# A two-layer decoder trunk on one core: second products of exact pairs contracted over all 128 rows instead of 64

## The chip, the core and the metric

The kernel runs on one core of a Trainium2 chip. The metric is the device time of one execution in microseconds (us); lower is better. TensorE does the matrix products, VectorE (DVE) and ScalarE (ACT) work on elements, GpSimd (POOL) does the rest of the element work, and SyncE (SP) issues most of the transfers.

## The reference, cut to what matters

A trunk of two layers on 1024 tokens of 1024 channels. The even layer projects the normed input and runs an RWKV-7 time mix, an S5 state space and an attention over 256 memory tokens; the odd layer runs a Mamba-2 branch, a latent attention (MLA) of 8 heads and the memory attention again. The three places that the change touches:

```python
# RWKV: decay and in-context rate from two latents of 64 channels each
log_w = -jax.nn.softplus(-(w0 + jnp.tanh(w_lat) @ w2)) - 0.5
iclr = jax.nn.sigmoid(a0 + a_lat @ a2)
...
# latent attention: scores of a block of 128 queries, 128 plain and 64 rotary channels a head
sc = (jnp.einsum('bqhd,bkhd->bhqk', q_nope[:, start:end], k_nope[:, :end])
      + jnp.einsum('bqhr,bkr->bhqk', q_pe[:, start:end], k_pe[:, :end]))
...
# memory attention: 4 heads of 64 channels, 256 keys
sc = jnp.einsum('bqhd,bmhd->bhqm', q, k).astype(jnp.float32) * HEAD_DIM ** -0.5
```

## The kernel before

**Exact pairs.** Float32 data are split into two parts, `hi + lo`, each short enough for TensorE's one-pass format (float32r). `split` (L402) does it with a copy on ACT (L404) and a subtraction on DVE (L405). A full product of 128 contracted rows is then three products: hi by hi, lo by hi, hi by lo.

Where the contraction has only 64 rows, one tile holds both parts: 64 of its 128 rows hold hi and the other 64 hold lo. Against a second tile that holds the hi part of the other factor in both halves, a single product over 128 rows gives hi by hi plus lo by hi. A second product adds hi by lo: in the kernel before it runs over the 64 rows that hold hi alone. Three places do so:

- LoRA of the RWKV branch (`rw_prep0`, L590 to L592): the latents `lt` against the weights `l2h` and then `l2l`, for two banks `pw` and `pa`. One unit is a head pair and half of the tokens; there are 16 units, so 32 second products of 64 rows and 512 columns. `lora` (L925 to L932) makes `l2h` with one copy on ACT and `l2l` with two subtractions on DVE of 64 rows by 128 (L931).
- Memory keys of the odd layer (`mem_branch` with `exact`, L1126 to L1135): queries `mqp` against `mkh` and then `mkr`. Eight rounds of (channel tile, half of the tokens, head), each with four pairs of 256 columns: 32 second products. `mkr` is made by two subtractions on DVE of 64 rows by 512 (L1097).
- Rotary part of the latent attention's scores (`mla_scores`, L2205): each bank gets `qnh` by `knh`, `qnh` by `knl`, `qnl` by `knh`, then `qp` by `kph` and, over 64 rows, `qp` by `kpl`. 64 blocks of 128 queries, the keys in one to three pieces: 104 second products of 128 to 512 columns. `kph` and `kpl` come from `split_load` and are full tiles.

**Order.** `Flow` (L159) is a planner that runs while the kernel is built. Streams of work share TensorE, each yields what its next step waits for, and the planner keeps its own clock: a product costs its columns at 2400 columns per us, whatever its rows are. The order of TensorE's instructions that comes out is fixed in the program. The dense projections (`dense`, L336) are one of the streams, and fill TensorE beside the RWKV branch, the memory branch and the latent attention. All matrix products have line L179 in the profile, the transposes L183, so the rows are told apart by tiles: out<-moving,stationary.

**Softmax of a block in the latent attention.** DVE adds the mask (L2210), reduces the maximum (L2211) and scales it (L2214), ACT takes the exponential (L2217), DVE the reciprocal (L2222), and ACT or DVE scales the probabilities (L2224, L2226). TensorE transposes them (`g<-ident,pe`), ACT and DVE split the result into `pth` and `ptl` (L2262, L2263), and TensorE multiplies by the values into `yps`.

**RWKV unit.** After LoRA come scans on DVE (L601) and exponentials, then triangular systems: `ga` goes to DRAM (`d_in`, L698), comes back as `ai`, one system per partition, and is inverted by chains of small POOL operations (L710, L712). The outputs pass `rw_out`, with a POOL operation on `ty` (L850) ahead of transposes on TensorE.

Of the kernel before, what the change touches and what calls it, by code (L numbers as in the profile page):

```python
# [10 lines left out]
F32 = mybir.dt.float32  # L11
F32R = mybir.dt.float32r
# [7 lines left out]
P = 128  # L20
# [9 lines left out]
# ---------------------------------------------------------------- host layout  # L30
# [24 lines left out]
def host_arrays(inp):  # L55
# [5 lines left out]
    # the S5 channels of a tile: by channel in the group, then by group  # L61
# [26 lines left out]
    # rows 32 r + q, column 2 c + i: channel q of group 2 r + i of tile c  # L88
# [23 lines left out]
    # by head pair, for both halves of the rows  # L112
# [46 lines left out]
class Flow:  # L159
    """The order of TensorE's work. Streams (generators) share it: the first one in rank that is  # L160
    ready goes on by a step. A stream yields what its next step waits for: a time in us from now,
    a PSUM tag and a number of its buffers, the name of an event, or a list of these."""
# [8 lines left out]
    # TensorE, in the order of the calls  # L171
# [13 lines left out]
    # PSUM buffers  # L185
# [11 lines left out]
    # events  # L197
# [27 lines left out]
    def run(self, until):  # L225
        """until the given streams have ended"""
# [19 lines left out]
class Item:  # L246
    """One product of the dense chain: out[m, tokens] = w^T x as three products of exact parts.
    x(h): (hi, lo) [128, kt, 512]; evac(h, psum) takes a half of the tokens. gen: any other work instead"""
# [8 lines left out]
class Tiles(list):  # L257
    """tiles [128, n], indexed as one [128, k, n] would be"""
# [6 lines left out]
class K:  # L265
# [4 lines left out]
    # ------------------------------------------------------------ constants  # L270
    def consts(self, es):
# [22 lines left out]
        # 1 - mu  # L294
# [10 lines left out]
    def new_banks(self, g, yps):  # L305
        """banks besides the dense chain's two"""
        if hasattr(self, "psum2"):
            self.psum2.close()
        self.psum2 = ExitStack()
        self.es.push(self.psum2)  # L310
        self.pbank = self.psum2.enter_context(self.tc.tile_pool(name="psum2", bufs=1, space=PSUM))
        self.flow.set_banks("g", g)
        self.flow.set_banks("yps", yps)
# [6 lines left out]
    # ------------------------------------------------------------ dense  # L320
    def load_w(self, parts, src, kt, m=P, pool=None):
        """generator: exact parts of a weight tile [128, kt, m], in pieces; yields the end of each"""
# [14 lines left out]
    def dense(self, items):  # L337
        """generator: the chain of dense products, the weights of the next ones loaded ahead"""
# [17 lines left out]
        def fill(n):  # L356
            """weights of the items up to the next but one, as far as there is room"""
            while at[0] < min(n, len(items) - 1) or live[0] < WB and at[0] < min(n + 2, len(items) - 1):
                at[0] = next(todo)
# [42 lines left out]
    def split(self, hi, lo, src):  # L402
        """hi + lo = src exactly, each with float32r's significand"""
        self.nc.scalar.copy(hi, src)  # L404
        self.nc.vector.tensor_tensor(lo, src, hi.bitcast(F32), A.subtract)  # L405

    def split_load(self, pool, hi, lo, src, n=HT):
        """exact parts of a DRAM tile [128, T]"""
# [5 lines left out]
    def gate2(self, g, ps):  # L414
        """g = 2 * silu(ps)"""
# [4 lines left out]
    def keep_evac(self, kind, dst):  # L420
        """evac of a projection to DRAM: 'gate', 'u' or 'copy'"""
        nc = self.nc

        def evac(h, ps):
            t = self.wp.tile([P, HT], F32, name="ev", bufs=2)
            if kind == "u":
                # tokens by place in the block, last first
# [11 lines left out]
    def put_y(self, kt, s, y):  # L439
        """y [128, n]: out-projection input kt, to DRAM"""  # L440
        self.nc.sync.dma_start(self.yd[kt, :, s], y)

    # ------------------------------------------------------------ norms
    def rstd(self, r, n, fill, scale_mat, rank_wait=0):
        """generator: r [128, n] = (mean over channels + eps)^-1/2 on every partition;
        fill(i, s): squares of one part of the channels for tokens s, or None after the last"""
# [14 lines left out]
    def norm_first(self, p, h, xhi, xlo):  # L461
        """generator: half of the input's tokens as exact parts, first without their norm (a factor per token, self.r0)
        for the products that come first, then with it"""
# [42 lines left out]
    def rw_consts(self, p):  # L506
# [16 lines left out]
        # per channel: w0 / 2, a0 / 2, 1 - k_a  # L523
# [6 lines left out]
        # identity start of the 32-row triangular inverses, in 4 interleaved column groups  # L530
        self.t0 = p.tile([P, 8, 32], F32, name="t0")
        nc.gpsimd.memset(self.t0, 0.0)
        for q in range(4):
            # t - 4 cc - q != 0 keeps 0, else 1
# [3 lines left out]
        # block diagonal holders of the inverses, zero outside what gets written  # L538
# [13 lines left out]
    def shift_evac(self, ci, dst, bd=None):  # L552
        """evac: p + (shift(p) - p) * mu, one half of the tokens each, to DRAM"""
# [15 lines left out]
    def rw_prep0(self, st, p, lat, l2, k, wk):  # L569
        """generator: channel-wise part of one head pair, one half of the tokens,  # L570
        as far as the triangular systems need it"""
# [18 lines left out]
        for i, (o, hs) in enumerate(((pw, slice(0, 64)), (pa, slice(64, 128)))):  # L590
            F.matmul(o, lhsT=l2h[:, i, :], rhs=lat[:, i], start=True, stop=False)
            F.matmul(o, lhsT=l2l[hs], rhs=lat[hs, i], start=False, stop=True)  # L592
# [23 lines left out]
        # K~, B~  # L616
        kr = wk.tile([P, 4, 2, P], F32, name="kr", bufs=3)
        nc.vector.tensor_tensor(kr[:, :, 0, :], b3(kh), e[:, :, 0:P], A.mult)
        # 1 / |k|^2, for both sides
# [5 lines left out]
        # the triangular part [s, t], transposed  # L625
# [5 lines left out]
    def pp_parts(self, x):  # L631
        """exact parts of x, where ce and cc of this unit were or will be"""
# [9 lines left out]
    def half_products(self, bm, kr, which, out):  # L642
        """out[s, b, h, t] = B~^T (K~ or R~), the latter masked to s <= t"""
# [6 lines left out]
        for h in range(2):  # L650
            if which == 0:
                # what the mask would clear is never read
# [5 lines left out]
    def rw_prep1(self, st, p, r, v, wk):  # L658
        """generator: the rest of it"""
# [6 lines left out]
        # bonus  # L666
# [3 lines left out]
        # token-major V, B~, K~'  # L670
# [18 lines left out]
    def rw_inv0(self, st, idx, wk):  # L689
        """inverses of the 32-blocks on the diagonal of I + A, one per partition,  # L690
        columns in 4 interleaved groups; transposed, into a block holder"""
# [21 lines left out]
        d_out = self.dr.tile([4, 8, 8, 4, 32], F32, name="d_out", bufs=2)  # i hb cc q t  # L713
# [5 lines left out]
    def rw_inv1(self, st, wk):  # L719
        """generator: the 32-block inverses grown to the inverse of the whole chunk"""  # L720
# [8 lines left out]
        # 32 -> 64  # L729
# [24 lines left out]
        # 64 -> 128  # L754
# [15 lines left out]
    def rw_seq(self, st, s0, i, wk):  # L770
        """generator: the chunks of one half in turn; y ends up in PSUM, token-major. i: which of the two at work"""
# [18 lines left out]
        for b in range(4):  # L790
# [33 lines left out]
            # the next chunk's start, in the scale of its middle  # L824
# [9 lines left out]
    def rw_out(self, p, hh, st, zd, wk):  # L834
        """generator: group norm (token-major), bonus, gate; result to DRAM"""
# [29 lines left out]
    def rsqrt(self, out, x, tmp, scale, eps):  # L865
        """out = (x scale + eps)^-1/2 on VectorE: a first guess from the exponent, then Newton's method"""
# [12 lines left out]
    def rw_items(self, np_, x, rd, zd, npairs=8):  # L879
        """the projections of the RWKV branch; the first two by halves of the tokens, with tiles from np_"""  # L880
# [32 lines left out]
    def rw_streams(self, cp, wk, rd, zd, npairs=8):  # L913
        """streams of the RWKV branch. The halves of two head pairs take turns, so that a half can begin
        before the one ahead of it has ended"""
# [9 lines left out]
        def lora(p):  # L925
            lr = self.pp.tile([P, 2, P], F32, name="l2", bufs=1)
            nc.sync.dma_start(lr, self.I["lora2"][p])
            l2 = (self.pp.tile([P, 2, P], F32R, name="l2h", bufs=1), self.pp.tile([P, P], F32R, name="l2l", bufs=1))
            nc.scalar.copy(l2[0], lr)
            for i, hs in enumerate((slice(0, 64), slice(64, 128))):  # L930
                nc.vector.tensor_tensor(l2[1][hs], lr[hs, i], l2[0][hs, i].bitcast(F32), A.subtract)  # L931
# [8 lines left out]
        def latents():  # L940
            """exact parts, stacked: tanh(w) hi | lo, a lo | hi; those of the first half stay"""
# [65 lines left out]
    # ------------------------------------------------------------ memory branch  # L1007
    def mem_norm(self, p, wait):
        """generator: the normed memory as exact parts, to DRAM"""
# [29 lines left out]
    def kv_items(self, layer, dst):  # L1039
        """keys (channel-major) and values of the normed memory, to dst (DRAM) [128, 4, 256]"""  # L1040
# [12 lines left out]
        # values by token: both token tiles in a bank, half of the contraction each  # L1053
# [27 lines left out]
    def mem_branch(self, layer, qd, zd, k0, p, wait, exact=False):  # L1081
        """generator: q (channel-major) and gates from DRAM -> out-projection inputs k0, k0 + 1.
        exact: products of exact parts, a head's high and low rows (or columns) side by side"""
# [5 lines left out]
        if exact:  # L1089
# [5 lines left out]
            nc.scalar.copy(kh, kl)  # L1095
            for h, hs in enumerate((slice(0, 64), slice(64, 128))):
                nc.vector.tensor_tensor(kr[hs, h], kl[hs, h], kh[hs, h].bitcast(F32), A.subtract)  # L1097
# [14 lines left out]
        def load(c, qh):  # L1112
# [3 lines left out]
            for h in range(2):  # L1116
                qs[c, qh, h] = q
                if exact:
                    # rows of the head's place high, the others low
# [4 lines left out]
        def scores(c, qh, h, q2):  # L1124
# [3 lines left out]
            for j in range(2):  # L1128
                o = slice(q2 * 256 + j * P, q2 * 256 + j * P + P)
                if exact:  # L1130
                    F.matmul(sc[:, j, :], lhsT=q[:, o], rhs=kh[:, h, c], start=True, stop=False)
                    F.matmul(sc[:, j, :], lhsT=q[hs, o], rhs=kr[hs, h, c], start=False, stop=True)
# [72 lines left out]
    def reduce_angle(self, k, out, x):  # L1205
        """out = x - 2 pi round(x / 2 pi)"""
# [7 lines left out]
    def sincos(self, s, c, r):  # L1214
        """r in [-pi, pi]; r is overwritten by its absolute value"""
# [5 lines left out]
    def s5_small(self, p):  # L1221
        """powers of the decays, e^(8 i theta)'s angle, |a|^8 and (a - 1) / lambda, to DRAM"""
# [37 lines left out]
        # f = (a - 1) / lambda  # L1260
# [25 lines left out]
    def s5_params(self, p, tp):  # L1286
# [13 lines left out]
        # b^ = f b  # L1300
        b16 = lambda ap: ap.unsqueeze(2).broadcast_to([P, 32, 16])
        # one column group more than there is: 32-wide slices of the last group stay inside
# [21 lines left out]
        # skip, as a part of the impulse response: row 32 r + q, column q  # L1324
# [9 lines left out]
    def s5_prep_x(self, q, ct, wk, st, free, wait):  # L1334
        """generator: what the state part of one 128-channel tile (8 channel groups) needs besides its input"""
# [1139 lines left out]
```

## Time and profile before

| | |
|---|---|
| median of 3 runs | 2826.01 us (2821.52 to 2829.27) |
| profiled execution, first to last instruction | 2839.6 us, 42364 instructions |
| PE busy, weight loads (PEld) busy | 2604.9 us (92%), 2058.7 us |
| DVE, ACT, POOL busy | 1787.5 us (63%), 1250.4 us (44%), 807.9 us (28%) |
| mean granted TensorE clock | 0.944 of full speed |

The page tells no more of the profiled execution than its span. The span is 13.6 us (0.5%) above the median of the runs, so stretches of it are taken as they stand and differences are carried to the median. A matmul's row shows when it starts; its end is modelled and includes the way through the array, so neighbours overlap in the rows. The time that one takes from the engine is read from start to start.

### The profile page before, as it was taken

Reading aid. Unit: us, or ns where it says so; the run is one execution under the profiler, and the core shown is the slowest. Engines: PE = TensorE matmul, PEld = TensorE weight load, DVE = VectorE, ACT = ScalarE, POOL = GpSimd, SP = SyncE. Lnnn points to the kernel's source line nnn. Section 1 sums busy time; section 2 is a strip of 40 time slices with the busy share of each in tenths; the row PEclk is TensorE's granted clock in tenths of the full one; section 3 lists DMA queues with packets and bytes.
Section 4 is the critical chain, followed back from the end, with each engine's and each line's share of the span. In section 5 each row is a group of like instructions: output and inputs, shape, how many; then the busy total and the mean of one; then the engine's idle time right before and its main releaser. Section 6 shows DMA issues by size and latency. Waiting matters only on the chain.

```text
span 2839.6 us, 42364 instructions
## 1 busy us (share of the span) xinstructions
PE 2604.9 (92%) x15058; PEld 2058.7 (72%) x15058; DVE 1787.5 (63%) x3383; ACT 1250.4 (44%) x2446; POOL 807.9 (28%) x1507
## 2 busy tenths in 40 slices
PE   7998899998998998888999998989899989999998
PEld 5776777776777776675678776767787767777786
DVE  8755556665655537787656457877734887776532
ACT  7433334333443333545533346435434445555443
POOL 4433544345435403354200111251420120000011
PEclk9998989999999989987999999999999999999999
DMA  4332223333232243454584564242455231113643
GB/s 156 115 100 77 84 77 90 95 86 93 85 100 68 70 127 134 107 162 150 160 274 137 162 189 122 79 107 77 113 163 190 88 103 62 44 45 98 197 134 100
DMA packets 263860, 328.27 MB, mean 116 GB/s; under 512 B 88017, under 2 KB 135249, under 8 KB 263137
## 3 DMA queue, kind: packets, MB, share of 16 engines
q1 hardware_dynamic: 260736, 319.39, 37.1%
q0 software_dynamic: 1280, 4.20, 0.4%
q8 instruction: 119, 1.95, 0.3%
q10 hardware_dynamic: 1632, 1.98, 0.2%
q14 instruction: 93, 0.75, 0.1%
HBM read 232.59 MB, written 92.90 MB: 115 GB/s over the span
## 4 chain that ended last, share of the span: by engine, by line
PE 50%; DMA 16%; DVE 15%; POOL 8%; issue 5%; ACT 4%; SPq 1%; DVEq 0%; ACTq 0%; POOLq 0%
PE mm L179 32%; PE g L179 12%; DMA ai<-d_in 5%; PE yps L179 3%; POOL ti L712 3%; POOL titmp L710 3%; PE g L183 2%; DVE wl L405 2%; DMA lm<-acd 1%; DMA gsz<-zd 1%; DMA w<-in_w_ev_out 1%; DMA d_in<-ga 1%; DMA spl<-yg 1%; DMA y<-yt 1%; DMA spl<-yd 1%
## 5 line engine op out<-in xcount | busy, mean ns | idle before, releaser
L405 DVE TENSOR_TENSOR wl<-w,wh 128x512 fp32r<-128x512 f32 (+2 forms) x410 | 285.0, 699 | 295.5 <-ACT wh L404 288.4
L404 ACT CAST wh<-w 128x512 fp32r<-128x512 f32 (+2 forms) x410 | 241.9, 594 | 429.4 <-PE mm L179 274.3
L179 PE MATMUL mm<-xhi,wh 128*128 128x512 f32 x832 | 371.0, 446 | 25.5 <-DVE ev L418 13.7
L179 PE MATMUL mm<-xlo,wh 128*128 128x512 f32 x832 | 344.2, 414 | 4.7 <-DVE xlo L496 2.4
L179 PE MATMUL mm<-xhi,wl 128*128 128x512 f32 x832 | 343.1, 412 | 0.0
L179 PE MATMUL mm<-x1h,wh 128*128 128x512 f32 (+1 forms) x608 | 254.4, 418 | 25.1 <-ACT craw L1822 14.3
L179 PE MATMUL mm<-x1h,wl 128*128 128x512 f32 (+1 forms) x608 | 243.4, 400 | 0.0
L179 PE MATMUL mm<-x1l,wh 128*128 128x512 f32 (+1 forms) x608 | 243.1, 400 | 0.0
L710 POOL TENSOR_TENSOR titmp<-ai,ti 128x60 f32<-128x60 f32 (+24 forms) x496 | 151.3, 305 | 313.8 <-DMA ai<-d_in 277.1
L179 PEld LDWEIGHTS mm<-xhi,wh 128*128 128x128 f32 x832 | 165.6, 199 | 82.7 <-issue 24.2
L179 PEld LDWEIGHTS mm<-xhi,wl 128*128 128x128 f32 x832 | 165.4, 199 | 40.5
L179 PEld LDWEIGHTS mm<-xlo,wh 128*128 128x128 f32 x832 | 166.6, 200 | 36.2 <-DVE xlo L474 5.0
L712 POOL TENSOR_TENSOR ti<-ti,titmp 128x60 f32<-128x60 f32 (+24 forms) x496 | 161.2, 325 | 38.2
L179 PEld LDWEIGHTS mm<-x1h,wh 128*128 128x128 f32 (+1 forms) x608 | 117.9, 194 | 59.0 <-ACT craw L1822 17.3
L179 PEld LDWEIGHTS mm<-x1l,wh 128*128 128x128 f32 (+1 forms) x608 | 117.6, 193 | 27.6 <-issue 3.6
L179 PEld LDWEIGHTS mm<-x1h,wl 128*128 128x128 f32 (+1 forms) x608 | 117.2, 193 | 27.0
L179 PE MATMUL mm<-yb,wh 128*128 128x512 f32 x320 | 102.4, 400 | 5.8 <-ACT yb L404 4.5
L785 DVE TENSOR_TENSOR gb<-g,m 128x256 f32<-128x256 f32 x128 | 49.5, 419 | 73.2 <-PE g L179 73.0
L799 ACT ACTIVATE sn<-s0c,fin 64x64 f32<-64x64 f32 x128 | 44.1, 345 | 106.4 <-DVE s0c L827 57.8
L1673 POOL TENSOR_TENSOR sq<-sq,sqt 128x512 f32<-128x512 f32 x14 | 18.0, 1289 | 245.7 <-DMA w<-in_w_ev_out 161.0
L2266 POOL CAST pth<-zero 128x128 fp32r<-128x128 f32 x32 | 11.3, 353 | 241.4 <-PE yps L179 179.8
L418 DVE SCALAR_TENSOR_TENSOR ev<-ev,mm 128x512 f32<-128x512 f32 x72 | 49.1, 682 | 45.5 <-ACT ev L417 45.2
(598 smaller groups left out, 6612.7 us busy)
## 6 DMA issues: line engine op xcount, KB each, us to landing
w<-in_w_ev_in SPq DMA_DIRECT2D x106, 256.0 KB
w<-in_w_od_in SPq DMA_DIRECT2D x82, 256.0 KB
w<-in_w_ev_out SPq DMA_DIRECT2D x64, 256.0 KB
w<-in_w_od_out SPq DMA_DIRECT2D x64, 256.0 KB
rd<-ev SPq DMA_DIRECT2D x50, 256.0 KB
spl<-yd SPq DMA_DIRECT2D x40, 256.0 KB
zod<-ev SPq DMA_DIRECT2D x36, 256.0 KB
ai<-d_in SPq DMA_DIRECT2D x16, 512.0 KB
```

Source lines behind the costliest of these rows:

```text
L179: return self._pe(self.nc.tensor.matmul(out, lhsT=lhsT, rhs=rhs, start=start, stop=stop, **kw), math.prod(rhs.shape[1:]), rhs.dtype)
L183: return self._pe(self.nc.tensor.transpose(out, src, ident), src.shape[0] // 2, F32)
L404: self.nc.scalar.copy(hi, src)
L405: self.nc.vector.tensor_tensor(lo, src, hi.bitcast(F32), A.subtract)
L418: nc.vector.scalar_tensor_tensor(g, g, 1.0, ps, A.add, A.mult)
L710: eng.tensor_tensor(tm, ai[:, s:s + 1, s + 1:32].broadcast_to([P, n, w]), ti[:, 0:n, s:s + 1].broadcast_to([P, n, w]), A.mult)
L712: eng.tensor_tensor(ti[:, 0:n, s + 1:32], ti[:, 0:n, s + 1:32], tm, A.subtract)
L785: nc.vector.tensor_tensor(gb[:, h], pgs[h], self.m2, A.mult)
L799: nc.scalar.mul(sg[hs], sc[hs, hs], g[hs])
L1673: nc.gpsimd.tensor_tensor(self.sq1, self.sq1, t, A.add)
L2266: nc.gpsimd.tensor_copy(t[:, n, 0:P], self.zero)
```

## The change

The second products of the three places contract over all 128 rows. Where the other factor's lo part stood in only the half of the rows that was used (`l2l`, `mkr`), it is now made for both halves, by `split`, as one subtraction of the whole tile; `kpl` was whole already. The products then also add lo by lo. `l2l` grows from 128 to 256 columns (512 bytes more in each partition). Nothing else in the program changes but comments.

```diff
@@ rw_prep0
-        for i, (o, hs) in enumerate(((pw, slice(0, 64)), (pa, slice(64, 128)))):
-            F.matmul(o, lhsT=l2h[:, i, :], rhs=lat[:, i], start=True, stop=False)
-            F.matmul(o, lhsT=l2l[hs], rhs=lat[hs, i], start=False, stop=True)
+        for i, o in enumerate((pw, pa)):
+            for j, w in enumerate((l2h, l2l)):
+                F.matmul(o, lhsT=w[:, i, :], rhs=lat[:, i], start=(j == 0), stop=(j == 1))
@@ lora
-            l2 = (self.pp.tile([P, 2, P], F32R, name="l2h", bufs=1), self.pp.tile([P, P], F32R, name="l2l", bufs=1))
-            nc.scalar.copy(l2[0], lr)
-            for i, hs in enumerate((slice(0, 64), slice(64, 128))):
-                nc.vector.tensor_tensor(l2[1][hs], lr[hs, i], l2[0][hs, i].bitcast(F32), A.subtract)
+            l2 = tuple(self.pp.tile([P, 2, P], F32R, name="l2" + n, bufs=1) for n in "hl")
+            self.split(*l2, lr)
@@ mem_branch
-            nc.scalar.copy(kh, kl)
-            for h, hs in enumerate((slice(0, 64), slice(64, 128))):
-                nc.vector.tensor_tensor(kr[hs, h], kl[hs, h], kh[hs, h].bitcast(F32), A.subtract)
+            self.split(kh, kr, kl)
@@ mem_branch, scores
-                    F.matmul(sc[:, j, :], lhsT=q[:, o], rhs=kh[:, h, c], start=True, stop=False)
-                    F.matmul(sc[:, j, :], lhsT=q[hs, o], rhs=kr[hs, h, c], start=False, stop=True)
+                    for x, k in enumerate((kh, kr)):
+                        F.matmul(sc[:, j, :], lhsT=q[:, o], rhs=k[:, h, c], start=(x == 0), stop=(x == 1))
@@ mla_scores
-        hs = slice((h % 2) * 64, (h % 2) * 64 + 64)
@@
-                for x, (l, r) in enumerate(((qh, kh), (qh, kl), (ql, kh), (qp, kph[:, u:v]), (qp[hs], kpl[hs, u:v]))):
+                for x, (l, r) in enumerate(((qh, kh), (qh, kl), (ql, kh), (qp, kph[:, u:v]), (qp, kpl[:, u:v]))):
```

## Rows read from the trace of the kernel before

**Rows 1.** Busy us of each engine (instructions), granted clock, DMA share, by stage.

```profile
74.00:934.00 860.00, 794.72 (x5825) 624.52 (x5824) 521.02 (x1160) 334.38 (x708) 385.16 (x1055) 0.93 0.31 88
...
2189.00:2269.00 80.00, 78.45 (x332) 59.06 (x330) 64.15 (x133) 40.10 (x105) 7.71 (x6) 0.96 0.31 104
...
2321.00:2608.00 287.00, 283.09 (x1596) 223.15 (x1594) 207.12 (x566) 159.65 (x393) 19.96 (x58) 0.99 0.19 59
```

**Rows 2.** Timeline of PE in the latent attention: start, us, operation, tiles.

```profile
2450.77 0.40 PE L179 MATMUL g<-knh,qnl 128*128 128x512 f32 x1
2451.01 0.40 PE L179 MATMUL g<-kph,qp 128*128 128x512 f32 x1
2451.33 0.50 PE L179 MATMUL g<-kpl,qp 64*128 64x512 f32 x1
2451.76 0.39 PE L179 MATMUL g<-knh,qnh 128*128 128x256 f32 x1
2451.99 0.28 PE L179 MATMUL g<-knl,qnh 128*128 128x256 f32 x1
...
2452.22 0.28 PE L179 MATMUL g<-kph,qp 128*128 128x256 f32 x1
2452.42 0.38 PE L179 MATMUL g<-kpl,qp 64*128 64x256 f32 x1
2452.73 0.39 PE L179 MATMUL yps<-pth,vh 128*128 128x256 f32 x1
2452.96 0.28 PE L179 MATMUL yps<-ptl,vh 128*128 128x256 f32 x1
```

**Rows 3.** Timeline of the weight loads there; in brackets idle time before.

```profile
2451.33 0.18 PEld L179 LDWEIGHTS g<-kpl,qp 64*128 64x128 f32 x1 [0.37 <-issue]
```

**Rows 4.** Products by tile: kpl, mkr, l2l; ns min/median/max, first and last start.

```profile
L179 PE MATMUL g<-kpl,qp x104: 322/440/792, 2321.9 to 2607.7; 64*128 64x512 f32 x40, 64*128 64x256 f32 x24, 64*128 64x384 f32 x24, 64*128 64x128 f32 x16
...
L179 PE MATMUL g<-mkr,mqp x32: 378/381/579, 2189.1 to 2268.9; 64*128 64x256 f32 x32
...
L179 PE MATMUL g<-lt,l2l x32: 491/498/502, 74.6 to 933.4; 64*128 64x512 f32 x32
```

**Rows 5.** Timeline of PE: first score product of a memory round, first transpose after.

```profile
2233.97 0.28 PE L179 MATMUL g<-mkh,mqp 128*128 128x256 f32 x1
...
2236.36 1.09 PE L183 MATMUL g<-ident,mpe 128*128 128x128 f32 x8
```

**Rows 6.** Timeline of PE at one LoRA unit: its first and last products, the next ones.

```profile
932.10 0.48 PE L179 MATMUL g<-lt,l2h 128*128 128x512 f32 x1
...
933.36 0.50 PE L179 MATMUL g<-lt,l2l 64*128 64x512 f32 x1
933.79 0.50 PE L179 MATMUL mm<-xhi,wh 128*128 128x512 f32 x1
934.13 0.40 PE L179 MATMUL mm<-xlo,wh 128*128 128x512 f32 x1
```

**Rows 7.** DVE groups: count, busy us, mean ns, idle before; RWKV stage, then latent attention.

```profile
L931 DVE TENSOR_TENSOR l2l<-l,l2h 64x128 fp32r<-64x128 f32 x30 | 11.4, 380 | 0.5 <-ACT l2h L929 0.2
...
L405 DVE TENSOR_TENSOR wl<-w,wh 128x256 fp32r<-128x256 f32 x7 | 3.0, 425 | 3.0 <-ACT wh L404 3.0
```

**Rows 8.** Waits of PE for other engines (us, times, longest): latent attention, RWKV stage.

```profile
PE g L183 <- ACT pe L2224: 2.2, 2, 1.7
...
PE g L183 <- POOL ty L850: 42.1, 12, 7.4
```

**Rows 9.** Chain that ended last, latent attention: start, us, what.

```profile
2583.42 0.31 ACT pe L2224
2583.78 0.33 PE g L183
```

**Rows 10.** Longest wait of PE between memory branch and latent attention (2269:2321).

```profile
PE mm L179 <- DVE qnl L2108: 8.0, 2, 7.6
```

**Rows 11.** Chain of 74 to 340 us, by line: shares.

```profile
by line: DMA ai<-d_in 20.3%; POOL ti L712 15.6%; POOL titmp L710 14.7%; issue 11.0%; PE mm L179 5.9%; PE g L179 4.8%; DMA d_in<-ga 3.6%; SPq L698 2.0%; DMA d_out<-ti 1.8%; DVE tb L586 1.6%; DVE ce L601 1.4%; PE yps L179 1.2%; DVE ev L565 1.
```

## Prediction

> **What bounds the kernel now.** I read the busy time by stage first. In the latent attention TensorE is busy 283.09 of 287 us, and in the memory branch 78.45 of 80; DVE is next with 207.12 and 64.15 [rows 1]. There the time is TensorE's, and what it is spared is time, up to the point where softmax or DVE comes too late. In the RWKV stage TensorE is busy 794.72 of 860 us [rows 1], and it waits: 42.1 us in 12 waits for the POOL operation on `ty` alone [rows 8]. The chain there runs mostly through the transfer of `ai` (20.3%) and the POOL inverse (15.6% and 14.7%), with 5.9% and 4.8% in TensorE's products [rows 11]. A saving on TensorE is worth less there.
>
> Then I read the timeline around the second products, start to start, since the ends are modelled. Undisturbed, a product of 512 columns takes 0.24 us (2450.77 to 2451.01), and two of 256 take 0.23 (2451.99 to 2452.22), 0.115 each [rows 2]. The reader should see three late steps around each product of 64 rows. `kph` to `kpl` takes 0.32, `kpl` to the next product 0.43 where its 512 columns need 0.24, and the next, with 256 columns, is followed after 0.23 instead of 0.115 [rows 2]. The weight load of `kpl` begins in the same instant as its product (2451.33), after 0.37 us in which no load ran, and the reason given is "issue", not another engine [rows 2, 3]. So its weights are not loaded behind the product ahead, and those of the full product behind it aren't either. It is the change between 64 and 128 rows that costs: `kph` has the same stationary tile `qp`, with 128 rows, and follows its neighbour after 0.24 us [rows 2].
>
> **The change part by part.** No product is added or removed, and none has more columns. The planner counts columns alone, so TensorE's order stays. What goes is the delay around 168 products: 104 with `kpl`, 32 with `mkr`, 32 with `l2l` [rows 4].
>
> *Latent attention.* With 512 columns and a product of 256 behind it: from 2451.01 to 2451.99 is 0.98 us, and undisturbed 2 x 0.24 + 0.115 = 0.595, so 0.385 is lost. With 256 columns: 2452.22 to 2452.96 is 0.74, against 3 x 0.115 = 0.345, so 0.395 [rows 2]. Both sizes lose the same, so I take 0.39 for all: 104 x 0.39 = 40.6 us.
>
> *Memory branch.* A round has eight products of 256 columns, full and half in turn: 2233.97 to 2236.36 is 2.39 us [rows 5], against 8 x 0.115 = 0.92. That is 1.47 us a round, and 8 rounds make 11.8 us.
>
> *LoRA.* From the first product of a unit to the second one behind it, 932.10 to 934.13, are 2.03 us for five products of 512 columns [rows 6], against 5 x 0.24 = 1.20. That is 0.83 us a unit, and 16 units make 13.3 us.
>
> Together TensorE is spared 65.7 us. No row shows these three products with 128 rows; the nearest are the first products of the same pairs, of the same columns, and they show no cost for rows. I take none.
>
> *DVE.* Two subtractions for `l2l` of 0.380 us each become one of 128x256, for which the nearest row has 0.425 [rows 7]: 2 x 0.380 - 0.425 = 0.335 less, in 16 units 5.4 us. Most of it lies beside the work of POOL and TensorE, so I count it at nothing and keep 5.4 as the upper bound. If that cover were gone, it would be a gain. For `mkr` two subtractions of 512 columns become one of 1024: the same columns, once in the program, taken as zero. ACT's copies stay. No transfer changes, and no wait is added: `l2l` and `mkr` came from DVE before, too.
>
> **What of the 65.7 us reaches the end.** *Latent attention.* TensorE now waits 2.2 us for scaled probabilities [rows 8], yet some arrive just in time: one ends at 2583.73, and its transpose starts at 2583.78 [rows 9]. With TensorE faster, such a block makes it wait for what was saved since its scores. 40.6 us over 64 blocks is 0.63 us a block. If none has slack for it, softmax sets the pace and nothing is gained. TensorE hardly waits now, so most have. I let one block in five give its 0.63 back: 13 x 0.63 = 8 us, which leaves 33. DVE isn't yet the bound: its 207.12 us stand against 287 - 33 = 254. Bounds: 20 (half the blocks give it back) to 40.6.
>
> *Memory branch.* DVE is busy 64.15 of 80 us [rows 1], and after the branch TensorE waits up to 7.6 us for `qnl` [rows 10], which lies behind the loads and splits that open the latent attention. Where that queue on DVE sets the end, a faster TensorE arrives earlier and waits longer. Bounds 0 and 11.8; I take 8, since TensorE is the fuller of the two.
>
> *RWKV.* LoRA stands on the loop of a unit (products, scans, `ga`, transfer, POOL inverse, `ty`, products), and so an earlier LoRA moves the POOL work too; but the loop turns on POOL and transfers more than on TensorE [rows 8, 11], and two units overlap. Bounds 0 and 13.3 + 5.4 = 18.7; I take half of 13.3, about 7.
>
> Sum: 33 + 8 + 7 = 48 us. The profiled span is 0.5% above the median of the runs, and I carry 48 over as it stands: 2826 - 48 = **2778 us**. Bounds: 20 + 0 + 0 = 20 us gives 2806, and 40.6 + 11.8 + 18.7 = 71 us gives 2755.
>
> **Rivals.**
> - *Waits take the place of the delays.* The softmax chain, DVE after the memory branch and POOL in the RWKV stage are all close behind TensorE, and most blocks give the time back. For it: 12 waits for `ty` [rows 8], and a block with 0.05 us of slack [rows 9]. Against it: hardly a wait in the two stages with 136 of the 168 products. Gain 9 to 30 us, about 2806. Chance 17%.
> - *All of it comes through*, DVE's too: 62 to 75 us, about 2757. For it: TensorE full in two stages [rows 1], and LoRA on the unit's loop. Against it: rows 9 and 11. Chance 12%.
> - *The change doesn't remove the delays*, because they come from the last product of a bank or from `lo` tiles, not from rows. Against it: in the memory round the full product behind each half one is late too, so that all eight take 0.3 us [rows 5], and `knl` is a `lo` tile without delay [rows 2]. No change, 2826. Chance 5%.
> - *Slower: the half-row product used half of the array and shared it with a neighbour.* Then the full one would take time that was free before: the columns of all 168 products, by the steps above (per 128 columns 0.06 us): 40 x 0.24 + 24 x 0.18 + 24 x 0.115 + 16 x 0.06 = 17.6 for `kpl`, 32 x 0.115 = 3.7 and 32 x 0.24 = 7.7, so 29 us more, 2855. It decides as soon as a half-row product starts before the columns of the one ahead are through. The rows show the contrary, 0.32 us after a product that needs 0.24 [rows 2]. Chance 2%; another 2% I leave to slower by the clock: 48 us would be eaten if as much of TensorE's work fell from 2.4 to 1.2 GHz, in stages where 0.93 to 0.99 is granted now [rows 1].
>
> This last mechanism is what the Trainium skill's page "TensorEngine Tiling (Array Packing)" recommends ("The Problem" and "When to Use Tiling"): at a contraction of 64 rows, tile the array by rows and run two products side by side, up to twice as fast. By that rule the change gives something up, and the sum would be the rival's 29 us. The trace doesn't agree for this kernel: its half-row products stand alone between full ones, and pay. The same page ("Key Properties") says that a change of the tiling mode drains TensorE; by that the third rival falls and the sum stays, and the late full products behind half ones agree [rows 2, 5].
>
> **How the numbers follow.** The likeliest is my sum, gain 30 to 62 us, 2764 to 2796, with 62%. About 0.3% (8.5 us) is what a measurement can tell from no change. Faster: 62 + 17 + 12 = 91%; within: 5%; slower: 4%. The range from 2755 to 2806 holds the likeliest case, about half of the first rival and most of the second: some 8 in 10.
>
> **What the profile after would show.** Right: `kpl`, `mkr` and `l2l` products with 128 rows, `kph` to `kpl` and `kpl` to the next in 0.24 us at 512 columns, weight loads without the idle 0.37; a memory round of 2.39 us down to about 0.95; five LoRA steps of 2.03 down to 1.2; the latent attention about 33 us shorter, with some 8 us more of waits for `pe` or `pth`; 16 subtractions for `l2l`. Wrong: the steps as short as said, but the stage as long, with TensorE's waits for ACT, DVE or POOL longer by the same sum (first rival); steps unchanged (third); or the order of work on DVE and ACT altered, so that waits move that I took as fixed, which would shift any stage by some us either way.

## The result and the profile after

The changed kernel took 2756.24 us (median of 4 runs, 2754.18 to 2763.8) against 2827.64 us before: ratio 0.9759, 95% interval 0.9732 to 0.9786, so 60 to 76 us faster. Measured twice more beside the experiments it came to 0.9794 (0.9774 to 0.9814) and 0.9795 (0.9769 to 0.9821), 2776.49 and 2773.55 us. The forecast was 2778, the range 2755 to 2806: the first measurement lies 1 us inside it.

A run's time is about 2 us over its span (2757.28 and 2755.3 for the profiled run after). The profiled execution before, with a span of 2839.6, was thus among the longest of its kind: 20 later runs of that kernel lie between 2819.74 and 2844.09. The two profiles differ by 84 us, which is more than the kernels do. Some 15 us of that lie between the LoRA stage and the memory branch, where the change touches only how `mkr` is made; before and after:

```profile
933.40:2189.00 1255.60, 1139.22 (x5998) 906.81 (x5997) 786.51 (x1208) 549.54 (x957) 321.81 (x323) 0.94 0.47 141
...
905.00:2146.00 1241.00, 1130.10 (x5998) 901.62 (x5997) 788.51 (x1205) 549.74 (x957) 318.64 (x325) 0.95 0.46 142
```

Over the profiles of all kernels below, this stretch takes 1241 to 1262 us. So a difference of ten or twenty us between two profiles is not yet a difference between two kernels. The latent attention is steadier: from first to last `kpl` product 282.7 to 288.1 us in five profiles without its part of the change, 255.5 to 256.9 in five with it as it stands in the changed kernel.

Busy time by stage after, cut at the same instructions (columns as in [rows 1]):

```profile
75.20:905.10 829.90, 769.41 (x5821) 614.02 (x5820) 518.34 (x1145) 333.51 (x706) 387.11 (x1052) 0.95 0.31 92
...
2146.00:2216.00 70.00, 66.62 (x334) 56.50 (x333) 63.63 (x134) 40.11 (x105) 6.77 (x5) 0.95 0.38 129
...
2269.00:2525.50 256.50, 246.24 (x1588) 219.37 (x1588) 203.09 (x564) 158.51 (x393) 20.65 (x58) 1.00 0.20 66
```

TensorE is still full in the latent attention, but now idles 10 of 256 us there, where it idled 4 of 287 [rows 1]. In the memory branch it is no fuller than DVE by much: 66.62 against 63.63 us.

The same pieces of the timeline of PE that were shown before, first the latent attention:

```profile
2384.83 0.39 PE L179 MATMUL g<-knh,qnl 128*128 128x512 f32 x1
2385.06 0.39 PE L179 MATMUL g<-kph,qp 128*128 128x512 f32 x1
2385.29 0.39 PE L179 MATMUL g<-kpl,qp 128*128 128x512 f32 x1
2385.51 0.28 PE L179 MATMUL g<-knh,qnh 128*128 128x256 f32 x1
2385.63 0.28 PE L179 MATMUL g<-knl,qnh 128*128 128x256 f32 x1
...
2385.87 0.28 PE L179 MATMUL g<-kph,qp 128*128 128x256 f32 x1
...
2386.23 0.28 PE L179 MATMUL yps<-ptl,vh 128*128 128x256 f32 x1
```

From `kph` to the second product behind `kpl` are now 0.57 us (2385.06 to 2385.63) instead of 0.98, and in the form of 256 columns 0.36 instead of 0.74 [rows 2]. A memory round and a LoRA unit:

```profile
2183.36 0.28 PE L179 MATMUL g<-mkh,mqp 128*128 128x256 f32 x1
...
2184.30 0.49 PE L183 MATMUL g<-ident,mpe 128*128 128x128 f32 x3
...
904.33 0.48 PE L179 MATMUL g<-lt,l2h 128*128 128x512 f32 x1
...
905.57 0.40 PE L179 MATMUL mm<-xlo,wh 128*128 128x512 f32 x1
```

The round takes 0.94 us instead of 2.39 [rows 5], the five LoRA steps 1.24 instead of 2.03 [rows 6]. So the delays are gone at all three places, in about the sizes that were forecast. By tiles, the answers to [rows 4]:

```profile
L179 PE MATMUL g<-kpl,qp x104: 273/336/398, 2268.9 to 2525.3; 128*128 128x512 f32 x40, 128*128 128x256 f32 x24, 128*128 128x384 f32 x24, 128*128 128x128 f32 x16
...
L179 PE MATMUL g<-mkr,mqp x32: 274/283/416, 2146.3 to 2215.6; 128*128 128x256 f32 x32
...
L179 PE MATMUL g<-lt,l2l x32: 389/393/398, 75.2 to 905.1; 128*128 128x512 f32 x32
```

Their first and last starts cut the stages in every kernel below. PE's waits, first in the latent attention, then ahead of it, then (last two) in the RWKV stage:

```profile
PE g L183 <- ACT pe L2219: 4.1, 2, 2.6
PE g L179 <- DVE lmx L2209: 1.7, 4, 0.6
PE yps L179 <- DVE lmx L2209: 1.5, 2, 0.8
...
PE mm L179 <- DVE qnl L2104: 8.1, 2, 7.6
...
PE g L183 <- POOL ty L850: 33.7, 12, 6.8
PE g L179 <- DVE xn L727: 13.6, 12, 4.2
```

### The profile page after: what moved, and what is told of

Its sections match the earlier page's. It is cut to its first block, busy times and chain, and to the rows that moved or that the text cites. A ratio compares the mean times of both kernels' runs of the same rounds, so it can differ in the third digit from the quotient of the medians.

```text
span 2755.3 us, 42347 instructions
## 1 busy us (share of the span) xinstructions
PE 2522.3 (92%) x15058; PEld 2036.7 (74%) x15058; DVE 1785.2 (65%) x3366; ACT 1250.2 (45%) x2446; POOL 804.7 (29%) x1507
## 5 line engine op out<-in xcount | busy, mean ns | idle before, releaser
L179 PEld LDWEIGHTS mm<-yb,wh 128*128 128x128 f32 x320 | 61.4, 192 | 20.7 <-ACT yb L404 4.4
```

What stands on the lines that cost most here:

```text
L179: return self._pe(self.nc.tensor.matmul(out, lhsT=lhsT, rhs=rhs, start=start, stop=stop, **kw), math.prod(rhs.shape[1:]), rhs.dtype)
```

## The experiments

Ratios are against runs of the kernel before in the same session, with 95% intervals.

**The three parts, each alone.** `e1_lora` has the hunks of `rw_prep0` and `lora`, `e2_memory` those of `mem_branch`, `e3_rotary` that of `mla_scores`. The parts for memory and rotary scores leave the order of work on all engines as it was. The LoRA part leaves TensorE's, and moves some DVE, ACT, POOL and SP work against each other.

> Only the LoRA part of the change: both products over 128 rows, one subtraction of 128x256 for l2l. Theory A (the delays at switches between 64 and 128 rows are the whole matter, and they come through where TensorE is full): 13 us less than before, 2814. Theory B (the new subtraction and the order of work on DVE and ACT that follows from it give most of what the RWKV stage gained, 28 us in the two profiles): 25 to 30 us less. My forecast on record was 7.

> Only the memory part: mkr whole, its 32 products over 128 rows; the order of work on all engines is that of before. Theory A: the eight rounds lose their 1.47 us each, all 11.8 us come through, 2815. Rival (DVE's queue after the memory branch sets the end): 0 to 5 us, with the wait for qnl after it longer by the rest.

> Only the rotary products with kpl over 128 rows; the order of work on all engines is that of before. Theory A: 104 x 0.39 = 40.6 us less in the latent attention, of which 28 to 40 reach the end, 2787 to 2799. Rival (softmax keeps the pace): under 25 us, with TensorE's waits for pe and pth up by 15 us or more.

| | ratio | us below before (2835.94) |
|---|---|---|
| LoRA part | 0.9926 (0.9902 to 0.9949) | 21 (14 to 28) |
| memory part | 0.9958 (0.9937 to 0.9979) | 12 (6 to 18) |
| rotary part | 0.9889 (0.9869 to 0.9908) | 31 (26 to 37) |
| sum | | 64 |

Where the time goes within a profile is told by the same rows of each kernel. The memory part's `mkr`, the rotary part's `kpl`, the LoRA part's `l2l`, first and last start:

```profile
L179 PE MATMUL g<-mkr,mqp x32: 274/283/416, 2191.5 to 2262.3; 128*128 128x256 f32 x32
```

```profile
L179 PE MATMUL g<-kpl,qp x104: 272/336/522, 2314.0 to 2569.5; 128*128 128x512 f32 x40, 128*128 128x256 f32 x24, 128*128 128x384 f32 x24, 128*128 128x128 f32 x16
```

```profile
L179 PE MATMUL g<-lt,l2l x32: 389/394/398, 74.7 to 921.2; 128*128 128x512 f32 x32
```

In `e2_memory` the longest wait for `qnl` behind the branch is the 7.6 us that it was [rows 10]:

```profile
PE mm L179 <- DVE qnl L2106: 8.0, 2, 7.6
```

The memory products take 70.8 us from the first to the last instead of 79.8, the rotary ones 255.5 instead of 285.8, the LoRA ones 846.5 instead of 858.8 [rows 4]. Three other profiled executions without the LoRA part have 854.0, 860.4 and 861.9. The rotary and the memory part follow theory A, and the rival that softmax keeps the pace falls. The LoRA part is between the theories: 21 us by the runs, where one said 13 and the other 25 to 30, and 12 us by the stage of its profile.

**The LoRA split alone.** `l2l` is made whole by one subtraction; the products stay over 64 rows.

```diff
-            F.matmul(o, lhsT=l2l[hs], rhs=lat[hs, i], start=False, stop=True)
+            F.matmul(o, lhsT=l2l[hs, i], rhs=lat[hs, i], start=False, stop=True)
@@ lora
+            l2 = tuple(self.pp.tile([P, 2, P], F32R, name="l2" + n, bufs=1) for n in "hl")
+            self.split(*l2, lr)
```

> Only the LoRA subtraction of the change: l2l made whole by one operation of 128x256, its products still over 64 rows with their delays; DVE, ACT, POOL and SP have the order of work of the LoRA part alone. Theory A: 0 to 5 us less than before, 2822 to 2828. Theory B: 12 to 17 us less. The difference to the LoRA part alone is the delays' own price: 13 us if they come through in full.

0.9969 (0.9948 to 0.9991): 9 us below before (3 to 15), between the theories again. Against the LoRA part, whose order of work is the same, 12 us are left for the 32 products over 128 rows. That would be nearly all of the 13.3 us of delays, but with the uncertainty of both figures it is 3 to 21. The traces are sharper: from the first product of a unit to the second one behind it, as in [rows 6], the 16 units take 31.8 us here and 19.2 in `e1_lora`, 12.6 less. PE's largest wait in the LoRA part's RWKV stage:

```profile
PE g L183 <- POOL ty L850: 42.8, 12, 8.6
```

It is what it was (42.1 us in 12 waits, [rows 8]): the time spared ahead of it didn't turn into waiting for POOL.

**Half-row products side by side.** In the kernel before, the first products of the memory keys and of the rotary pair are cut to 64 rows too (lo by hi is left out there).

```diff
-                    F.matmul(sc[:, j, :], lhsT=q[:, o], rhs=kh[:, h, c], start=True, stop=False)
+                    F.matmul(sc[:, j, :], lhsT=q[hs, o], rhs=kh[hs, h, c], start=True, stop=False)
@@ mla_scores
-    (qp, kph[:, u:v]), (qp[hs], kpl[hs, u:v])
+    (qp[hs], kph[hs, u:v]), (qp[hs], kpl[hs, u:v])
```

> The kernel before, with the first products of the memory keys and of the rotary scores cut to 64 rows as well (lo by hi is left out there), so that half-row products stand beside half-row products. Theory A (a switch between 64 and 128 rows costs, not the half-row product): a memory round of eight takes about 0.92 + 0.4 = 1.3 us instead of 2.39 and saves some 8 us in all, and the delay around the rotary pair stays at 0.39; the time is 5 to 10 us below before. Rival (each half-row product costs by itself): the round stays at 2.4 us or longer and the rotary delay doubles to 0.8; 30 to 50 us above before.

0.9975 (0.9961 to 0.9988): 7 us below before (3 to 11), as expected; from the first to the last `mkr` product it takes 72.4 us (2186.7 to 2259.1) instead of 79.8. A memory round and a rotary pair on its PE timeline:

```profile
2225.95 0.38 PE L179 MATMUL g<-mkh,mqp 64*128 64x256 f32 x1
2226.17 0.28 PE L179 MATMUL g<-mkr,mqp 64*128 64x256 f32 x1
2226.29 0.28 PE L179 MATMUL g<-mkh,mqp 64*128 64x256 f32 x1
...
2227.10 0.55 PE L183 MATMUL g<-ident,mpe 128*128 128x128 f32 x3
...
2445.93 0.39 PE L179 MATMUL g<-knh,qnl 128*128 128x512 f32 x1
2446.25 0.49 PE L179 MATMUL g<-kph,qp 64*128 64x512 f32 x1
2446.58 0.39 PE L179 MATMUL g<-kpl,qp 64*128 64x512 f32 x1
2446.91 0.45 PE L179 MATMUL g<-knh,qnh 128*128 128x384 f32 x1
2447.19 0.34 PE L179 MATMUL g<-knl,qnh 128*128 128x384 f32 x1
```

Eight half-row products in a row follow each other in 0.12 us, and the round takes 1.15 us (2225.95 to 2227.10): 0.94 for all full, 2.39 for full and half in turn. Two half-row products in the rotary pair lose together 0.38 us (2445.93 to 2447.19 is 1.26, undisturbed 3 x 0.235 + 0.175), as much as one did. So the price is that of a switch between 64 and 128 rows, and not of a half-row product. The Trainium skill states on its page "TensorEngine Tiling (Array Packing)", "Key Properties", that changing the tiling mode drains TensorE. These rows agree, and with those of the change they give the price: 0.36 to 0.41 us for a switch and the switch back.

In one place this kernel shows more. The first two rounds of the memory branch belong to two heads, one with rows 0 to 63 and one with rows 64 to 127, and here no full products stand between them (x2: two products in one row of the view):

```profile
2187.32 0.58 PE L179 MATMUL g<-mkh,mqp 64*128 64x256 f32 x2
2187.53 0.58 PE L179 MATMUL g<-mkr,mqp 64*128 64x256 f32 x2
2187.75 0.58 PE L179 MATMUL g<-mkh,mqp 64*128 64x256 f32 x2
2187.96 0.59 PE L179 MATMUL g<-mkr,mqp 64*128 64x256 f32 x2
2188.35 0.41 PE L179 MATMUL g<-mkh,mqp 64*128 64x256 f32 x1
2188.56 0.41 PE L179 MATMUL g<-mkr,mqp 64*128 64x256 f32 x1
```

At a granted clock of 0.50, where it is 1.00 in the rows above, one product at a time takes 0.21 us (2188.35 to 2188.56), yet eight take 1.03 (2187.32 to 2188.35): products over different halves of the rows ran at the same time. The kernel before had no such neighbours in the three places.

**Does DVE's time for `l2l` set a LoRA unit's pace?** Two kernels change it from both sides. `e6_lora_products` is the LoRA part with four subtractions of 64x128; `e11_lora_keep` is the changed kernel with the split weights kept for the second half of the tokens, so that half of the subtractions are gone:

```diff
@@ lora, e6_lora_products
+            for i in range(2):
+                for hs in (slice(0, 64), slice(64, 128)):
+                    nc.vector.tensor_tensor(l2[1][hs, i], lr[hs, i], l2[0][hs, i].bitcast(F32), A.subtract)
@@ lora, e11_lora_keep
+            if p in kept:
+                return kept.pop(p)
+            lr = self.pp.tile([P, HT], F32, name="ta", bufs=1)[:, 0:2 * P].rearrange("p (i m) -> p i m", i=2)
+            l2 = kept[p] = tuple(self.pp.tile([P, 2, P], F32R, name="l2" + n, bufs=2) for n in "hl")
```

> The LoRA part alone, but with l2l made by four subtractions of 64x128 instead of one of 128x256: about 4 x 0.33 - 0.38 = 0.9 us more on DVE in each of 16 units, 15 us in all. If DVE's time for l2l is on the path of a unit: 10 to 15 us slower than the LoRA part alone, so within 0.4% of before. If DVE's time is covered: like the LoRA part alone, 0.6 to 0.8% below before. The order of some DVE, ACT and SP work differs too, which may add some us either way.

> The changed kernel, with the split LoRA weights of a head pair kept for its second half of the tokens, so that 8 of the 16 subtractions of l2l, 8 copies and 8 transfers are gone (the raw weights take the place of another scratch tile). If DVE's time for l2l is on a unit's path, as the LoRA split alone (9 us below before) and the four subtractions (16 us above the LoRA part) suggest: 8 x 0.36 = 3 us or more below the changed kernel, up to 8. If the order of work was the matter there: within 3 us either way.

More subtractions cost 20 us (12 to 28): 0.9995 (0.9979 to 1.001), where the LoRA part has 0.9926. Added up over the traces, DVE spends 18.6 us more on `l2l` (25.9 against 7.3); 10 to 15 had been expected. Fewer of them gained nothing: 2780.36 us against 2773.55 for the changed kernel in the same session (0.9813 with 0.9786 to 0.984, against 0.9795), 7 us more with intervals that overlap. But that kernel hardly tests the question, as its row beside that of the changed kernel shows:

```profile
L405 DVE TENSOR_TENSOR l2l<-l,l2h x16: 360/362/1487, 27.8 to 864.8; 128x256 fp32r<-128x256 f32 x16
...
L405 DVE TENSOR_TENSOR l2l<-ta,l2h x8: 415/426/1483, 28.0 to 778.7; 128x256 fp32r<-128x256 f32 x8
```

Each subtraction takes longer there, so DVE is spared 1.5 us (7.4 to 5.9) and not the 3 that were counted. The split alone spares it some 6 us (7.3, where three kernels with two subtractions have 12.9 to 14.1), and 9 in the time. So two of the three changes are of the size of DVE's own, and the third is too small to tell; but all three also shift DVE, ACT and SP work, and the last takes another scratch tile. Whether the 9 us of the split come from DVE's time or from the order of work stays open.

**Can the rest of the rotary gain be had?** The planner's delay from scores to transposes, `MP`, in the changed kernel; it also changes the order of TensorE's products:

```diff
-MP = 6
+MP = 8    # e8_after_mp8; 5 in e10_after_mp5
```

> The changed kernel with the planner's delay from a block's scores to its transposes raised from 6 to 8 us. Theory: the 11 us of the rotary delays that didn't reach the end went into TensorE's waits for softmax (pe, lmx, ptl: 9 us); a longer planned distance removes them: 3 to 8 us below the changed kernel. Rival: the distance moves the waits elsewhere, to the score banks or the end of the stage: within 3 us of the changed kernel.

> The changed kernel with the planner's delay from a block's scores to its transposes lowered from 6 to 5 us (8 us cost 10 us). Theory: 6 is right for the softmax chain's length, and a shorter distance leads to longer waits for pe: 3 to 10 us above the changed kernel. Rival: the waits after the change are at the score banks and at yps, and a shorter distance serves them: 2 to 6 us below.

> The changed kernel again, on the same chip as the parts. Theory A (the parts add up): 0.74 + 0.42 + 1.11 = 2.27% below before, 64 us; the first measurement had 2.41%.

> The changed kernel once more, on the same chip as the two versions of it: 2.0 to 2.4% below before.

Neither is better. With 8 the kernel takes 2786.77 us against 2776.49 for the changed kernel, 10 us more where 3 to 8 less were expected; with 5 it takes 2783.04 against 2773.55, as the theory said, though the intervals overlap (0.9794 to 0.9846 and 0.9769 to 0.9821). From the first to the last `kpl` product are 268.5 and 264 us, where the changed kernel has 256.4:

```profile
L179 PE MATMUL g<-kpl,qp x104: 272/338/415, 2286.1 to 2554.6; 128*128 128x512 f32 x40, 128*128 128x256 f32 x24, 128*128 128x384 f32 x24, 128*128 128x128 f32 x16
```

```profile
L179 PE MATMUL g<-kpl,qp x104: 272/336/628, 2296.5 to 2560.3; 128*128 128x512 f32 x40, 128*128 128x256 f32 x24, 128*128 128x384 f32 x24, 128*128 128x128 f32 x16
```

PE's waits in that stage, with 8 and then with 5:

```profile
PE g L183 <- ACT pe L2212: 7.6, 9, 1.8
PE yps L179 <- DVE ptl L2258: 5.7, 7, 1.4
```

```profile
PE g L183 <- ACT pe L2219: 5.2, 1, 5.2
PE g L183 <- DVE pe L2221: 3.8, 3, 1.3
```

The longer distance moves the waits to other transposes and to `ptl`, the shorter one lengthens those for `pe`. The parts had been measured on another chip than the changed kernel here, so each is compared with the kernel before in its own session. The two measurements of the changed kernel itself gave 2.06 and 2.05% below before, a little under the 2.27% of the parts' sum and inside its uncertainty.

## Why the prediction was right, and where its sizes were off

**The cause.** Right: the delays belonged to the switch between 64 and 128 rows, a product over 128 rows costs no more than one over 64, and the delays vanished by about the amounts worked out. The third rival (delays of `lo` tiles or last products) falls by the change itself and by the half-row experiment. The rival that half-row products shared the array falls by the changed kernel's rows, where the full products take 0.12 and 0.23 us. Such sharing does exist, as `e5_pairs64` shows, but between products over different halves, and the second products had only full ones beside them.

**Rotary scores: 33 of 40.6 us forecast, 31 measured alone.** From first to last `kpl` product the changed kernel has 256.4 us (2268.9 to 2525.3) against 285.8, so 29 us, and `e3_rotary` has 255.5, so 30. A part of the rest went where the prediction put it, into TensorE's waits for softmax: in the stage they add up to 3.3 us before, 7.3 in `e3_rotary` and 9.4 after. Another part was never there. `e3_rotary` has the order of the kernel before, so its products can be matched one by one. The three steps around each second product got shorter by 0.38 us in the median, but a third of them by less than 0.33, and all 104 together by 35.6 us, waits left out. The step from two readings to "0.39 for all" thus counted 5 us too many. With the 4 us of longer waits that makes 9 of the 10 us that `e3_rotary` misses.

**Memory branch: 8 of 11.8 forecast, 12 measured (6 to 18).** The time alone doesn't tell 12 from 8. But the rows don't bear out the discount, that DVE's queue would turn an earlier TensorE into a longer wait for `qnl`. The wait was 7.6 us [rows 10] and stayed 7.6, with the whole change and in `e2_memory`, whose eight rounds take 11.3 us less than before. The profile gives a reason as far as rows can: the stage from the last `mkr` to the first `kpl` product kept its length (53.0 us before, 53.3 after), so the queue on DVE that opens the latent attention seems to have begun earlier, together with TensorE.

**RWKV: 7 forecast, 21 measured (14 to 28).** This term was mis-sized most, in two places. Half of the 13.3 us was written off because POOL and transfers dominate the chain [rows 11]; the units' steps got 12.6 us shorter, the time 12 (3 to 21), and the wait for `ty` didn't grow. That fits a loop through TensorE, the transfer and POOL, which is shortened by whatever is taken from any of them; no run tests the loop itself. And the shorter subtraction was counted at nothing with 5.4 us as its bound, where the split alone gave 9 (3 to 15), for a cause that stays open between DVE's time (some 6 us less) and the order of work that the smaller program got. The profiles can't place all of the 21 us: the stage is 12 us shorter in `e1_lora` than before, and its length differs by 8 us (854.0 to 861.9) between profiles in which nothing of it was changed.

**The sum.** 48 forecast; the parts measured alone make 64, and the whole measured 58 us in the later sessions and 68 (60 to 76) in the first. By the first measurement the second rival, "all of it comes through", has the closer time (2757), but not the mechanism: of the 40.6 us counted for the rotary part a quarter doesn't reach the end, in part for waits. That 2778 is close to the later measurements is partly luck, since the kernel before took 7 to 11 us more in those sessions than the 2826 from which 48 was taken, and the change gave 58; and the first measurement is outside the 2764 to 2796 that was called likeliest. In the first session's profile the RWKV stage took 829.9 us at a granted clock of 0.95, in the later two profiles of the same kernel 848.1 and 843.6 us at 0.93 and 0.94. Two of them:

```profile
74.30:922.40 848.10, 780.76 (x5821) 623.08 (x5820) 517.52 (x1145) 333.83 (x706) 387.49 (x1052) 0.93 0.32 90
```

```profile
74.50:918.10 843.60, 776.52 (x5821) 620.00 (x5820) 518.33 (x1145) 333.43 (x706) 386.34 (x1052) 0.94 0.32 90
```

The work is the same, and PE is busy 7 to 11 us longer in them. Why the clock was higher in the first session isn't shown. The three later sessions were on three different chips, so chip and session can't be told apart.

## What to carry to other kernels

Look for products that use half of the rows between products that use all of them: the delay shows as a weight load that starts with its own product, with "issue" as the reason of its idle time, and a late product behind it. If the unused rows can be filled with data that do no harm, do it, or place half-row products side by side; the price is per switch. Two that use different halves of the rows can even run at the same time, as one stretch of `e5_pairs64` shows; whether that would beat filling the rows here was not tried. And when such a delay is on a loop of several engines, count it in full at first, and write it off only where a row shows a wait that will grow.

## What the runs showed of the hardware that was not expected

A product over 64 rows beside others of 64 rows follows in 0.12 us with 256 columns, the same as one over 128 rows, so the number of rows costs nothing by itself. Products over different halves of the rows ran at the same time, eight in the time of five. The same kernel, unchanged, differs between sessions by 20 us (2756.24 and 2776.49), about 0.7%; the kernel before differed by 5 to 10 us (2827.64, 2832.78, 2835.94, 2837.33).
